# Weight splits of 1024 columns and adaLN modulation in units of 1024 columns, in a two-layer hybrid mixer step

## The chip, the cores and the metric

The kernel runs on one core of a Trainium2 chip. The metric is the time of one execution on the device in microseconds; the median of three runs before the change is 1260.74 us (1260.21 to 1266.0). TensorE is PE in the profile (PEld its weight loads), VectorE is DVE, ScalarE is ACT, SyncE is SP; SP issues the large loads.

## The reference

Two token groups (128 prompt tokens, 256 sample tokens) pass through two layers of width D = 2048. Each layer's modulation is a matrix product of a conditioning vector with `w_mod`; its three parts of 2048 columns are shift, scale and gate.

```python
def trunk_layer(x, cvec, l, p, rope=None, ctx_k=None, ctx_v=None):
    shift, scale, gate = jnp.split(jax.nn.silu(cvec) @ p['w_mod'][l] + p['b_mod'][l], 3, axis=-1)
    h = rmsnorm(x, p['norm_g'][l]) * (1 + scale) + shift
    (f_x, f_g, p_x, p_g, q, k, v, a_g, c_a, c_b, c_g) = jnp.split(h @ p['w_in'][l], N_IN_CHUNKS, axis=-1)
    y_f = fourier_mix(f_x, p['w_fourier'][l]) * jax.nn.silu(f_g)
    y_p = pool_mix(p_x, p['w_pool'][l], p['pool_scale'][l]) * jax.nn.silu(p_g)
    y_c = conv_module(c_a, c_b, ...) * jax.nn.silu(c_g)
    ...
    y_a = o.transpose(0, 2, 1, 3).reshape(b, s, D_BRANCH) * jax.nn.silu(a_g)
    y = jnp.concatenate([y_f, y_p, y_a, y_c], axis=-1) @ p['w_out'][l]
    return x + gate * y, k, v
```

The prompt group has one conditioning vector and the sample group another, so every modulation is computed for two vectors. All data are float32. After the second layer a last rmsnorm gives the outputs; the prompt's keys and values are outputs too.

## The kernel before

**Matrix products.** The 384 tokens of both groups stand in the free dimension, and D in 16 blocks of 128 partitions (KC = 16). A weight tile is 512 KB, [128 partitions x 2 blocks x 512 columns], in a pool of five buffers (`rawp`). `wtile` (L219) loads it and `halves` (L203) splits each half of 512 columns into a rounded part `hi` (ACT, `copy_a`, L115) and a rest `lo` (DVE, `tt`, L106), in pools of six buffers each. `mm3` (L428) then does three matmuls of 384 columns for each 128 x 128 block: `hh`x`hi` (L429), `hl`x`hi` (L430), `hh`x`lo` (L431), where `hh` and `hl` are the two parts of the activation (`yh`, `yl` in the output projection). A tile has 24 such matmuls (`main_tile`, L433). In the trace each of them is one record where it reads rounded data, and two where it reads plain float32.

**Stages of a layer.** Eleven chunks of 512 columns of `w_in`, the mixers between them, then the output projection with `w_out`. Layer 0's first four chunks run differently: they are taken k-group by k-group (nine groups, four tiles each) while the modulation of layer 0 is still being computed; `make_h` makes the activation of a group (`ht`, `hh`, `hl`), and DVE adds each tile's result from PSUM into `acc`. Which instruction comes when on an engine is settled by the scheduler of the Tile framework; loads and splits go into it with priority (`ahead`, L200).

**Modulation.** It is doled out beside the main work. `pump` (L341) runs after each weight tile and issues what is due of two lists.
- *PE items* (`mod_item`, L247): a load of `mraw` and, for each block of 128 rows and each of four groups of 32 columns of the PE array, one matmul (L271) with the conditioning vectors (`cmod`) as the stationary side, into PSUM `mod`. Two items are issued at a time (BP = 2). An item of two blocks with 512 columns has eight matmuls of 128 columns; one of one block with 1024 columns has four of 256. At a unit's end a transpose (`T`) and `mod_store` follow.
- *DVE side items* (`side_item`, L307): a load of `sraw` [128 x 2 x 512], then for each of the two blocks and both vectors one DVE instruction of 512 columns into `macc` (L321 for the first block, L109 after it). When all 16 blocks are in, eight matmuls with ones (`mds`, L331), 128 columns each, sum over the partitions, then a transpose and `mod_store` follow. `macc` and `sraw` are taken from the pool `X` of four buffers in layer 0, and from the pool `H` in the output projection.

`share` (L374) assigns units to the two lists. For layer 1's shift and scale (L814) there are eight units of 512 columns: the first three go to PE, NS = 5 to DVE. For layer 1's gate (L941) there are four, two of them (NG = 2) on DVE; the two on PE are merged into one wide unit (`mod_wide`). How fast the lists go is set by tile counts (PE0, PE1, DV0, DV1 in L64).

**The layer boundary.** After layer 0's last output tile TensorE does the last `mds`, the first wide unit of layer 1's gate (16 matmuls), sums of squares (`st`, L412), a broadcast (`bc`, L407), and then layer 1's first matmuls as soon as `hh` is there.

Of the kernel before, what the change touches and what calls it, by code (L numbers as in the profile page):

```python
# [14 lines left out]
P = 128  # L15
# [40 lines left out]
def mixer_step(  # L56
# [8 lines left out]
    NS, NG = 5, 2  # L65
# [13 lines left out]
    hip = ctx.enter_context(tc.tile_pool(name="hip", bufs=6))  # L79
    lop = ctx.enter_context(tc.tile_pool(name="lop", bufs=6))  # L80
# [56 lines left out]
    nc.vector.memset(cmod, 0.0)  # L137

# [64 lines left out]
    def halves(raw, src, widths):  # L203
        flat = raw.rearrange("p a b -> p (a b)") if len(raw.shape) == 3 else raw
        hs, ls = [], []
        with ahead():
            nc.sync.dma_start(out=src[0], in_=src[1])
        for i, w in enumerate(widths):
            hi = hip.tile([P, 512], F32R, tag="hi", name=nm("hi"))
            lo = lop.tile([P, 512], F32R, tag="lo", name=nm("lo"))  # L210
            r = flat[:, 512 * i:512 * i + w]
            with ahead():
                copy_a(hi[:, :w], r)
                tt(lo[:, :w], r, hi[:, :w].bitcast(F32), ALU.subtract)
            hs.append(hi)
            ls.append(lo)
        return hs, ls

    def wtile(src, nk=None, shape=(P, 2, 512)):  # L219
        nk = nk or shape[1]  # L220
        n = shape[2]
        raw = rawp.tile(list(shape), F32, tag="raw", name=nm("raw"))
        hs, ls = halves(raw, (raw[:, :nk], src), [min(512, nk * n - o) for o in range(0, nk * n, 512)])

        def part(ts):
            def at(j, cs=slice(0, n)):
                i, o = divmod(j * n, 512)
                return ts[i][:, o + cs.start:o + cs.stop]
            return at
        return part(hs), part(ls)  # L230
# [70 lines left out]
    def side_items(l, kind, b0):  # L301
        return [(l, kind, b0, k0) for k0 in range(0, KC, 2)]
# [4 lines left out]
    def side_item(l, kind, b0, k0):  # L307
        pool = side_pool[0]
        key = (l, kind, b0)
        if k0 == 0:  # L310
            side_acc[key] = gtile(pool, "macc", (P, 2, 512))
        acc = side_acc[key]
        raw = gtile(pool, "sraw", (P, 2, 512))
        c0 = MOD.index(kind) * D + b0 * P
        with ahead():
            nc.sync.dma_start(out=raw, in_=w_src("w_mod", l, k0, c0))
        for j in range(2):
            for v in range(2):
                cv = cmod[:, k0 + j, v:v + 1]
                if k0 + j == 0:  # L320
# [758 lines left out]
```

## Time and profile before

| | |
|---|---|
| median of the runs | 1260.74 us (1260.21, 1260.74, 1266.0) |
| the profiled execution | 1261.78 us, span 1260.0 us, mean granted TensorE clock 0.993 |
| TensorE busy | 98% of the span |
| VectorE busy | 72% |
| ScalarE busy | 44% |
| DMA | 251.85 MB moved, mean 200 GB/s |

The span is what the instructions of the profiled execution cover; the execution's own time is 1.78 us longer. Busy time is the union of an engine's records, and a group's mean is the length of one record: records of an engine overlap, so the distance between two starts (the pitch) is shorter than the mean. In the timeline a row of several records gives the start of the first, the time from there to the end of the last, and their count.

### The profile page before, as it was taken

What the parts mean: (1) busy time and instruction counts of PE and PEld (TensorE: products, weight loads), DVE (VectorE), ACT (ScalarE), POOL (GpSimd) and SP (SyncE); (2) the same over time, 40 slices, a digit from 0 to 9 for tenths busy, and PEclk for the clock granted to TensorE, in tenths of its full rate; (3) what the DMA queues carried; (4) which work ended last, traced back from release to release, by engine and by line L of the source; (5) the groups of instructions that cost most, each with busy time, mean ns of one, the idle gap of its engine ahead of it and who ended that gap; (6) DMA issues with size and microseconds to landing.
All of it is one profiled execution on the core that took longest, in us unless ns stands there. A gap on an engine that the chain in (4) does not pass through costs nothing.

```text
span 1260.0 us, 22153 instructions
## 1 busy us (share of the span) xinstructions
PE 1232.5 (98%) x8600; PEld 1155.2 (92%) x8600; DVE 912.3 (72%) x1773; ACT 553.7 (44%) x1116; POOL 2.1 (0%) x34
## 2 busy tenths in 40 slices
PE   7999999999999999999999999999999999999995
PEld 7789998798998999999998999979999999999995
DVE  0578777999975966998977559998455795647452
ACT  3423233345447545433235533334554765344442
POOL 0000000000000000000000000000000000000000
PEclk9999999999999999999999999999999999999998
DMA  5878887553446765888954444444323573545322
GB/s 222 317 295 324 289 328 269 189 186 113 139 150 226 273 241 185 314 307 318 329 198 176 165 153 159 153 159 147 103 84 118 175 243 117 192 162 189 118 68 100
DMA packets 70712, 251.85 MB, mean 200 GB/s; under 512 B 7760, under 2 KB 8912, under 8 KB 70608
## 3 DMA queue, kind: packets, MB, share of 16 engines
q1 hardware_dynamic: 70608, 250.45, 56.6%
q8 instruction: 67, 1.10, 0.4%
q14 instruction: 37, 0.30, 0.1%
HBM read 243.08 MB, written 7.34 MB: 199 GB/s over the span
## 4 chain that ended last, share of the span: by engine, by line
PE 92%; DVE 3%; DMA 2%; ACT 1%; issue 1%; SPq 0%; DVEq 0%; ACTq 0%
PE mm L429 25%; PE mm L430 23%; PE mm L431 23%; PE mod L271 5%; PE mm L460 2%; PE mm L461 2%; PE mm L462 2%; PE ssq L166 2%; DVE lo L106 1%; DMA raw<-in_w_in_dram 1%; PE sp L430 1%; PE sp L429 1%; PE scs L634 1%; PE sp L431 1%; PE aso L658 1%; PE fb L701 1%
## 5 line engine op out<-in xcount | busy, mean ns | idle before, releaser
L115 ACT ACTIVATE hi<-raw 128x512 fp32r<-128x512 f32 x498 | 308.4, 630 | 539.5 <-PE mm L430 340.8
L106 DVE TENSOR_TENSOR lo<-raw,hi 128x512 fp32r<-128x512 f32 x498 | 337.4, 687 | 209.4 <-ACT hi L115 198.9
L429 PE MATMUL mm<-hh,hi 128*128 128x384 f32 x1280 | 441.0, 345 | 5.4 <-ACT hh L112 3.9
L430 PE MATMUL mm<-hl,hi 128*128 128x384 f32 x1280 | 433.0, 338 | 0.0
L431 PE MATMUL mm<-hh,lo 128*128 128x384 f32 x1280 | 430.9, 338 | 0.4 <-DVE lo L106 0.4
L429 PEld LDWEIGHTS mm<-hh,hi 128*128 128x128 f32 x1280 | 241.0, 188 | 26.7 <-issue 11.4
L430 PEld LDWEIGHTS mm<-hl,hi 128*128 128x128 f32 x1280 | 242.1, 189 | 1.4 <-issue 0.6
L431 PEld LDWEIGHTS mm<-hh,lo 128*128 128x128 f32 x1280 | 241.5, 189 | 1.5 <-DVE lo L106 1.2
L429 PE MATMUL mm<-yh,hi 128*128 128x384 f32 x512 | 173.4, 340 | 0.3 <-DVE xr L109 0.3
L430 PE MATMUL mm<-yl,hi 128*128 128x384 f32 x512 | 172.4, 337 | 0.0
L431 PE MATMUL mm<-yh,lo 128*128 128x384 f32 x512 | 172.3, 337 | 0.0
L109 DVE SCALAR_TENSOR_TENSOR macc<-sraw,cmod,macc 128x512 f32<-128x512 f32 x210 | 147.4, 743 | 7.0 <-DMA sraw<-in_w_mod_dram 7.0
L109 DVE SCALAR_TENSOR_TENSOR cacc<-u,cst,cacc 128x399 f32<-128x399 f32 x232 | 146.5, 631 | 7.6 <-ACT cacc L112 3.2
L429 PEld LDWEIGHTS mm<-yh,hi 128*128 128x128 f32 x512 | 96.2, 188 | 3.9 <-issue 3.3
L430 PEld LDWEIGHTS mm<-yl,hi 128*128 128x128 f32 x512 | 96.3, 188 | 0.0
L431 PEld LDWEIGHTS mm<-yh,lo 128*128 128x128 f32 x512 | 96.2, 188 | 0.0
L106 DVE TENSOR_TENSOR acc<-acc,mm 128x384 f32<-128x384 f32 x128 | 65.4, 551 | 26.8 <-PE mm L431 26.7
L271 PE MATMUL mod<-mraw,cmod 128*32 128x128 f32 (+2 forms) x1920 | 76.8, 294 | 0.4 <-DVE T L276 0.4
L271 PEld LDWEIGHTS mod<-mraw,cmod 128*32 128x32 f32 x1920 | 48.2, 112 | 22.8 <-issue 14.6
L112 ACT ACTIVATE hh<-ht,AB 128x128 fp32r<-128x128 f32 x64 | 26.9, 450 | 25.8 <-DVE ht L109 25.6
L460 PE MATMUL mm<-hi,hh 128*128 128x512 f32 x96 | 38.3, 399 | 0.0
L461 PE MATMUL mm<-lo,hh 128*128 128x512 f32 x96 | 38.0, 396 | 0.0
(205 smaller groups left out, 954.9 us busy)
## 6 DMA issues: line engine op xcount, KB each, us to landing
raw<-in_w_in_dram SPq DMA_DIRECT2D x172, 512.0 KB, 4.3
mraw<-in_w_mod_dram SPq DMA_DIRECT2D x136, 512.0 KB, 4.4
raw<-in_w_out_dram SPq DMA_DIRECT2D x64, 512.0 KB, 4.3
sraw<-in_w_mod_dram SPq DMA_DIRECT2D x56, 512.0 KB, 5.6
xT<-in_x_dram SPq DMA_DIRECT2D x4, 768.0 KB, 7.2
xr<-in_x_dram SPq DMA_DIRECT2D x4, 768.0 KB, 6.5
xd<-xr SPq DMA_DIRECT2D x4, 768.0 KB, 6.3
xr<-xd SPq DMA_DIRECT2D x4, 768.0 KB, 6.0
```

Source lines behind the costliest of these rows:

```text
L106: (eng or nc.vector).tensor_tensor(out=out, in0=a, in1=b, op=op)
L109: nc.vector.scalar_tensor_tensor(out=out, in0=a, scalar=s, in1=b, op0=op0, op1=op1)
L112: nc.scalar.activation(out=out, in_=a, func=func, **kw)
L115: nc.scalar.activation(out=out, in_=a, func=AF.Copy, scale=scale)
L166: nc.tensor.matmul(ssq[:, t:t + 1], lhsT=xsq[:, b, t * P:(t + 1) * P], rhs=ones[:, 0:1], start=g == 0 and b == 0 and t == 0, stop=g == 3 a ...
L271: nc.tensor.matmul(ps[qs, 0:nb * 32].rearrange("p (b n) -> p b n", n=32), lhsT=cmod[:, k0 + j, :], rhs=raw[:, j, :, qs], start=(k0 + j == ...
L429: nc.tensor.matmul(ps, lhsT=wh, rhs=ah, start=start, stop=False)
L430: nc.tensor.matmul(ps, lhsT=wh, rhs=al, start=False, stop=False)
L431: nc.tensor.matmul(ps, lhsT=wl, rhs=ah, start=False, stop=stop)
L460: nc.tensor.matmul(ps3[t], lhsT=hh[g][:, kb, ts], rhs=hi(j), start=st, stop=False)
L461: nc.tensor.matmul(ps3[t], lhsT=hh[g][:, kb, ts], rhs=lo(j), start=False, stop=False)
L462: nc.tensor.matmul(ps3[t], lhsT=hl[g][:, kb, ts], rhs=hi(j), start=False, stop=sp)
```

## The change

The split of a weight tile becomes one `hi` and one `lo` instruction of up to 1024 columns, with pools of three buffers of 1024 columns in place of six of 512. Modulation units for layer 1 have 1024 columns: four units for shift and scale, NS = 3 of them on DVE and one on PE, and two for the gate, NG = 1 on DVE and one on PE. A side item covers one block of 128 rows by 1024 columns: one load of 512 KB, two DVE instructions of 1024 columns; the sums for the two vectors stand in two tiles of the pool instead of one. At a unit's end eight matmuls of 256 columns have `pick` as the stationary side (a column of ones at the vector's place), and the two vectors accumulate into one tile.

```diff
--- before.py
+++ after.py
@@ -62,7 +62,7 @@
     nc = tc.nc
     PRIO = 1000
     PE0, PE1, DV0, DV1 = 78, 45, 61, 34
-    NS, NG = 5, 2
+    NS, NG = 3, 1
     WF, WP, WQ, WC = 3, 2, 3, 0
     YC1, YC2, YC3, YT = 1, 4, 1, 2
     NB1, NB2 = 2, 2
@@ -76,8 +76,8 @@
     pbp = ctx.enter_context(tc.tile_pool(name="pbp", bufs=4))
     cap = ctx.enter_context(tc.tile_pool(name="cap", bufs=1))
     rawp = ctx.enter_context(tc.tile_pool(name="rawp", bufs=5))
-    hip = ctx.enter_context(tc.tile_pool(name="hip", bufs=6))
-    lop = ctx.enter_context(tc.tile_pool(name="lop", bufs=6))
+    hip = ctx.enter_context(tc.tile_pool(name="hip", bufs=3))
+    lop = ctx.enter_context(tc.tile_pool(name="lop", bufs=3))
     kvp = ctx.enter_context(tc.tile_pool(name="kvp", bufs=2))
     tiny = ctx.enter_context(tc.tile_pool(name="tiny", bufs=2))
     tmpp = ctx.enter_context(tc.tile_pool(name="tmpp", bufs=2))
@@ -135,6 +135,10 @@
     nc.vector.memset(eps_t, EPS)
     cmod = one.tile([P, KC, 32], F32, tag="cmod", name="cmod")
     nc.vector.memset(cmod, 0.0)
+    pick = one.tile([P, 2, 32], F32, tag="pick", name="pick")
+    nc.vector.memset(pick, 0.0)
+    for v in range(2):
+        nc.vector.memset(pick[:, v, v:v + 1], 1.0)
 
 
     in_order = ExitStack()
@@ -200,34 +204,24 @@
     def ahead():
         return tc.high_priority(offset=PRIO if prio[0] else 0)
 
-    def halves(raw, src, widths):
-        flat = raw.rearrange("p a b -> p (a b)") if len(raw.shape) == 3 else raw
-        hs, ls = [], []
-        with ahead():
-            nc.sync.dma_start(out=src[0], in_=src[1])
-        for i, w in enumerate(widths):
-            hi = hip.tile([P, 512], F32R, tag="hi", name=nm("hi"))
-            lo = lop.tile([P, 512], F32R, tag="lo", name=nm("lo"))
-            r = flat[:, 512 * i:512 * i + w]
-            with ahead():
-                copy_a(hi[:, :w], r)
-                tt(lo[:, :w], r, hi[:, :w].bitcast(F32), ALU.subtract)
-            hs.append(hi)
-            ls.append(lo)
-        return hs, ls
-
     def wtile(src, nk=None, shape=(P, 2, 512)):
         nk = nk or shape[1]
         n = shape[2]
+        w = nk * n
         raw = rawp.tile(list(shape), F32, tag="raw", name=nm("raw"))
-        hs, ls = halves(raw, (raw[:, :nk], src), [min(512, nk * n - o) for o in range(0, nk * n, 512)])
-
-        def part(ts):
+        hi = hip.tile([P, 1024], F32R, tag="hi", name=nm("hi"))
+        lo = lop.tile([P, 1024], F32R, tag="lo", name=nm("lo"))
+        r = raw.rearrange("p a b -> p (a b)")[:, :w]
+        with ahead():
+            nc.sync.dma_start(out=raw[:, :nk], in_=src)
+            copy_a(hi[:, :w], r)
+            tt(lo[:, :w], r, hi[:, :w].bitcast(F32), ALU.subtract)
+
+        def part(t):
             def at(j, cs=slice(0, n)):
-                i, o = divmod(j * n, 512)
-                return ts[i][:, o + cs.start:o + cs.stop]
+                return t[:, j * n + cs.start:j * n + cs.stop]
             return at
-        return part(hs), part(ls)
+        return part(hi), part(lo)
 
     def w_src(name, l, k0, c0, nk=2, n=512):
         def rows(a):
@@ -299,39 +293,38 @@
         return mod_items(l, ((kind, k0, 8),), 1)
 
     def side_items(l, kind, b0):
-        return [(l, kind, b0, k0) for k0 in range(0, KC, 2)]
+        return [(l, kind, b0, k) for k in range(KC)]
 
     side_acc = {}
     side_pool = ["X"]
 
-    def side_item(l, kind, b0, k0):
+    def side_item(l, kind, b0, k):
         pool = side_pool[0]
         key = (l, kind, b0)
-        if k0 == 0:
-            side_acc[key] = gtile(pool, "macc", (P, 2, 512))
+        if k == 0:
+            side_acc[key] = [gtile(pool, "macc", (P, 1024)) for _ in range(2)]
         acc = side_acc[key]
-        raw = gtile(pool, "sraw", (P, 2, 512))
+        raw = gtile(pool, "sraw", (P, 1, 1024))
         c0 = MOD.index(kind) * D + b0 * P
         with ahead():
-            nc.sync.dma_start(out=raw, in_=w_src("w_mod", l, k0, c0))
-        for j in range(2):
-            for v in range(2):
-                cv = cmod[:, k0 + j, v:v + 1]
-                if k0 + j == 0:
-                    nc.vector.tensor_scalar(out=acc[:, v, :], in0=raw[:, j, :], scalar1=cv, scalar2=None, op0=ALU.mult)
-                else:
-                    stt(acc[:, v, :], raw[:, j, :], cv, acc[:, v, :], ALU.mult, ALU.add)
-        if k0 + 2 == KC:
+            nc.sync.dma_start(out=raw, in_=w_src("w_mod", l, k, c0, 1, 1024))
+        for v in range(2):
+            cv = cmod[:, k, v:v + 1]
+            if k == 0:
+                nc.vector.tensor_scalar(out=acc[v], in0=raw[:, 0, :], scalar1=cv, scalar2=None, op0=ALU.mult)
+            else:
+                stt(acc[v], raw[:, 0, :], cv, acc[v], ALU.mult, ALU.add)
+        if k + 1 == KC:
             del side_acc[key]
-            ps = sm("mds", (P, 2, 4, 32))
-            av = acc.rearrange("p v (b n) -> p v b n", n=P)
-            for v in range(2):
-                for q in range(4):
-                    qs = slice(32 * q, 32 * q + 32)
-                    nc.tensor.matmul(ps[qs, v], lhsT=ones[:, 0:32], rhs=av[:, v, :, qs])
-            T = one.tile([P, 2, 4, 32], F32, tag="S", name=nm("T"))
-            nc.vector.transpose(out=T.rearrange("p v b n -> p (v b n)"), in_=ps.rearrange("p v b n -> p (v b n)"))
-            mod_store(l, kind, b0, 4, T[:, :, :, 0].rearrange("p v b -> p b v"))
+            ps = sm("mds", (P, 8, 32))
+            for q in range(4):
+                qs = slice(32 * q, 32 * q + 32)
+                for v in range(2):
+                    nc.tensor.matmul(ps[qs], lhsT=pick[:, v, :], rhs=acc[v].rearrange("p (b n) -> p b n", n=P)[:, :, qs],
+                                     start=v == 0, stop=v == 1)
+            T = one.tile([P, 8, 32], F32, tag="S", name=nm("T"))
+            nc.vector.transpose(out=T.rearrange("p b n -> p (b n)"), in_=ps.rearrange("p b n -> p (b n)"))
+            mod_store(l, kind, b0, 8, T[:, :, 0:2])
 
     fill = {"pe": [], "dve": []}
     rate = {"pe": 0.0, "dve": 0.0}
@@ -373,12 +366,8 @@
 
     def share(l, units, n_side):
         n_pe = len(units) - n_side
-        for i in range(n_pe):
-            kind, b0 = units[i]
-            if i % 2 == 0 and i + 1 < n_pe and units[i + 1] == (kind, b0 + 4):
-                fill["pe"].extend(mod_wide(l, kind, b0))
-            elif not (i % 2 and units[i - 1] == (kind, b0 - 4)):
-                fill["pe"].extend(mod_items(l, ((kind, b0, 4),), 2))
+        for kind, b0 in units[:n_pe]:
+            fill["pe"].extend(mod_wide(l, kind, b0))
         for kind, b0 in units[n_pe:]:
             fill["dve"].extend(side_items(l, kind, b0))
 
@@ -811,7 +800,7 @@
             in_order.close()
             make_lambda()
             fill["pe"].extend(mod_wide(0, "gate", 0)[8:] + mod_wide(0, "gate", 8))
-            share(1, [(kind, b0) for b0 in range(0, KC, 4) for kind in ("shift", "scale")], NS)
+            share(1, [(kind, b0) for b0 in range(0, KC, 8) for kind in ("shift", "scale")], NS)
             set_rate("pe", PE0)
             src = {ci: (lambda b, ci=ci: acc[ci][:, b, :]) for ci in lead}
             th = glu_tanh(src[C_B], acc[C_B])
@@ -938,7 +927,7 @@
         pump(flush=True)
         rate["pe"] = rate["dve"] = 0.0
         if not final:
-            share(1, [("gate", b0) for b0 in range(0, KC, 4)], NG)
+            share(1, [("gate", b0) for b0 in range(0, KC, 8)], NG)
             pe_mods(NB1)
         stat = tots[1]
         if not final:
```

The scheduler orders the new program anew. In it the line numbers are smaller: `mod` is L265, `mds` L323, `mm3` L418 to L420, `st` L401, `bc` L396.

VectorE in the first four chunks of layer 0, around one weight tile, before (`ht` is the scaled activation of a block, `acc` the sum of a chunk in SBUF, the last two rows the two halves of one tile's split):

```order
L109 SCALAR_TENSOR_TENSOR ht_936<-xT_120,AB_204,bcs_218 128x128
L109 SCALAR_TENSOR_TENSOR ht_936<-xT_120,AB_204,bcs_218 128x256
L106 TENSOR_TENSOR acc_467<-acc_467,mm_835 128x384
L106 TENSOR_TENSOR acc_467<-acc_467,mm_836 128x384
L106 TENSOR_TENSOR acc_467<-acc_467,mm_837 128x384
L106 TENSOR_TENSOR acc_467<-acc_467,mm_838 128x384
L106 TENSOR_TENSOR lo_929<-raw_926,hi_928 128x512
L106 TENSOR_TENSOR lo_933<-raw_926,hi_932 128x512
```

Now:

```order
L109 SCALAR_TENSOR_TENSOR ht_924<-xT_124,AB_208,bcs_222 128x128
L109 SCALAR_TENSOR_TENSOR ht_924<-xT_124,AB_208,bcs_222 128x256
L109 SCALAR_TENSOR_TENSOR ht_931<-xT_124,AB_208,bcs_222 128x128
L109 SCALAR_TENSOR_TENSOR ht_931<-xT_124,AB_208,bcs_222 128x256
L106 TENSOR_TENSOR acc_471<-acc_471,mm_831 128x384
L106 TENSOR_TENSOR acc_471<-acc_471,mm_832 128x384
L106 TENSOR_TENSOR acc_471<-acc_471,mm_833 128x384
L106 TENSOR_TENSOR acc_471<-acc_471,mm_834 128x384
L106 TENSOR_TENSOR lo_920<-raw_918,hi_919 128x1024
```

Two `ht` of the next block have moved ahead of the four additions, and one `lo` of 1024 columns stands for two.

TensorE at the layer boundary, from the end of layer 0's output projection on, before (`mds` sums a side unit, `mod` is the gate's unit, `st` the sums of squares, `bc` the broadcast):

```order
L331 MATMUL mds_7217<-macc_6810,ones 32x128 x8
L331 MATMUL mds_7278<-macc_7229,ones 32x128 x8
L271 MATMUL mod_7293<-mraw_7291,cmod 32x256
L412 MATMUL st_7159<-ones,xsq_7205 128x1 x3
L271 MATMUL mod_7293<-mraw_7291,cmod 32x256 x3
L271 MATMUL mod_7293<-mraw_7298,cmod 32x256 x4
L271 MATMUL mod_7293<-mraw_7304,cmod 32x256 x4
L271 MATMUL mod_7293<-mraw_7310,cmod 32x256 x4
L407 MATMUL bc_7324<-dg_7320,ones 128x384
```

Now, from the last two of eight `mds` rows on (`macc_6304` and `macc_6305`, the sums of the two vectors, alternate):

```order
L323 MATMUL mds_6577<-macc_6304,pick 32x256
L323 MATMUL mds_6577<-macc_6305,pick 32x256
L265 MATMUL mod_6592<-mraw_6590,cmod 32x256 x4
L265 MATMUL mod_6592<-mraw_6597,cmod 32x256 x4
L265 MATMUL mod_6592<-mraw_6603,cmod 32x256
L401 MATMUL st_6487<-ones,xsq_6527 128x1 x3
L265 MATMUL mod_6592<-mraw_6603,cmod 32x256 x3
L265 MATMUL mod_6592<-mraw_6609,cmod 32x256 x4
L396 MATMUL bc_6623<-dg_6619,ones 128x384
```

One side unit ends there instead of two, and the three `st` have moved from behind the first `mod` to behind the ninth.

## Rows read from the trace of the kernel before

**Rows 1.** Page, head and part 1: engine busy us, share of the span, instructions.

```profile
span 1260.0 us, 22153 instructions
...
PE 1232.5 (98%) x8600; PEld 1155.2 (92%) x8600; DVE 912.3 (72%) x1773; ACT 553.7 (44%) x1116; POOL 2.1 (0%) x34
```

**Rows 2.** Page, part 4: the chain that ended last, by engine.

```profile
PE 92%; DVE 3%; DMA 2%; ACT 1%; issue 1%; SPq 0%; DVEq 0%; ACTq 0%
```

**Rows 3.** TensorE's waits: who for, us in total, times, longest.

```profile
PE ssq L166 <- ACT xsq L112: 6.8, 1, 6.8
PE mm L429 <- ACT hh L112: 3.9, 3, 1.9
...
PE mm L429 <- DVE acc L106: 1.3, 1, 1.3
...
PE mm L431 <- DVE lo L106: 0.4, 1, 0.4
```

**Rows 4.** Groups by line and form: shapes, count | busy us, mean ns | idle before.

```profile
L106 DVE TENSOR_TENSOR lo<-raw,hi 128x512 fp32r<-128x512 f32 x498 | 337.4, 687 | 209.4 <-ACT hi L115 198.9 <-PE mm L431 7.8 <-PE mm L430 1.4
...
L109 DVE SCALAR_TENSOR_TENSOR macc<-sraw,cmod,macc 128x512 f32<-128x512 f32 x210 | 147.4, 743 | 7.0 <-DMA sraw<-in_w_mod_dram 7.0
...
L106 DVE TENSOR_TENSOR rsh<-rsh,cst 128x1024 f32<-128x1024 f32 x4 | 4.9, 1215 | 0.0
```

**Rows 5.** TensorE's timeline, three bursts: start us, us, line, count.

```profile
509.47 0.65 PE L331 MATMUL mds<-macc,ones 128*32 128x128 f32 x16
...
536.16 0.34 PE L431 MATMUL mm<-yh,lo 128*128 128x384 f32 x1
...
537.44 0.44 PE L429 MATMUL mm<-yh,hi 128*128 128x384 f32 x1
...
710.51 0.34 PE L429 MATMUL mm<-hh,hi 128*128 128x384 f32 x1
710.68 0.34 PE L430 MATMUL mm<-hl,hi 128*128 128x384 f32 x1
710.86 0.34 PE L431 MATMUL mm<-hh,lo 128*128 128x384 f32 x1
711.13 1.07 PE L271 MATMUL mod<-mraw,cmod 128*32 128x256 f32 x16
712.13 0.45 PE L429 MATMUL mm<-hh,hi 128*128 128x384 f32 x1
```

**Rows 6.** Timelines of VectorE and TensorE in layer 0's output projection.

```profile
585.23 6.05 DVE L109 SCALAR_TENSOR_TENSOR macc<-sraw,cmod,macc 128x512 f32<-128x512 f32 x9
591.58 1.29 DVE L106 TENSOR_TENSOR lo<-raw,hi 128x512 fp32r<-128x512 f32 x2 [0.30 <-ACT hi L115]
...
597.70 0.44 PE L429 MATMUL mm<-yh,hi 128*128 128x384 f32 x1
```

**Rows 7.** Timelines of VectorE and TensorE, layer 0's first four chunks.

```profile
78.80 0.48 DVE L109 SCALAR_TENSOR_TENSOR ht<-xT,AB,bcs 128x256 f32<-128x256 f32 x1
...
81.30 1.29 DVE L106 TENSOR_TENSOR lo<-raw,hi 128x512 fp32r<-128x512 f32 x2
...
82.05 0.97 PE L431 MATMUL mm<-hh,lo 128*128 128x384 f32 x4
```

**Rows 8.** Window 500:660 (us; PE, PEld, DVE, ACT, POOL busy, clock, DMA), and side loads.

```profile
500.00:660.00 160.00, 159.70 (x1178) 153.36 (x1176) 143.45 (x253) 54.45 (x94) 0.35 (x6) 1.00 0.83 297
...
DMA to landing us min/median/max: 3.6/6.4/8.6
```

**Rows 9.** Layer boundary: TensorE's timeline, and the window's row.

```profile
676.03 1.07 PE L429 MATMUL mm<-hh,hi 128*128 128x384 f32 x4 [1.89 <-ACT hh L112]
...
678.25 0.52 PE L430 MATMUL mm<-hl,hi 128*128 128x384 f32 x1
678.57 0.52 PE L431 MATMUL mm<-hh,lo 128*128 128x384 f32 x1
...
660.00:680.00 20.00, 18.08 (x141) 15.66 (x141) 12.38 (x34) 8.26 (x17) 0.00 (x0) 0.92 0.60 219
```

## Prediction

> **What bounds the kernel now.** The reading goes from the page's engine line to the chain of waits, from there to TensorE's own waits, and only then to single stretches. TensorE (PE) is busy for 1232.5 of 1260.0 us [rows 1], and the chain that ended last lies on it for 92% [rows 2]. What it waits for by name is one startup wait of 6.8 us, 3.9 us in three pieces for ScalarE's (ACT's) `hh`, and little else; VectorE's (DVE's) `lo` accounts for 0.4 us, once [rows 3]. So the time is, to about 2%, TensorE's stream of matmuls at their pitch. A change shortens the kernel if it takes matmuls out of that stream or removes one of the few waits; a shorter list on DVE or ACT shortens nothing by itself.
>
> The profiled execution took 1261.78 us (span 1260.0 and 1.78 around it), 1.04 above the median of 1260.74. What follows are differences on that execution, and I set them against the median.
>
> **1. Splits of 1024 columns.** Each full weight tile had two `hi` and two `lo` instructions of 512 columns, now one of each. A 512-column `lo` takes 687 ns, and a subtract or multiply of 1024 columns in the trace takes 1215 ns [rows 4], so a tile's `lo` costs 1.22 us where it cost 1.37: 0.15 us x 249 tiles (498 halves) = 37 us of busy time by these means, less back to back. `hi` should fall likewise. All of that lies beside TensorE, so the saving is worth nothing. The cost is that `lo` comes later, and what hides it is how early `lo` is. In the busiest stretch a pair of `lo` is done at 592.87, and the tile's matmuls begin at 597.70 [rows 6], 4.8 us later. A `lo` that starts only when the whole `hi` is done, and is itself one piece, comes some 0.6 + 0.5 us later, and a buffer that is given back by the tile comes back half a tile later (12 matmuls of 0.17 us [rows 5], 2.1 us). Together 3.2 us, which fits. Were it gone, each tile would wait.
>
> It does not fit at the start, where layer 0's first four chunks run k-group by k-group and DVE adds every tile's result into SBUF. Two `lo` start at 81.30, and the first matmul that reads one runs at 82.05 [rows 7]: TensorE is there when the first half is done. One `lo` of 1024 columns is ready 1.22 us after its start, not about 0.7, so 0.5 later. The order of instructions also puts two more `ht` ahead of it, 0.48 us for the one of 256 columns [rows 7] and less for the one of 128, about 0.8 together; and it puts a mod item of 16 records (0.65 us, as the burst of that size [rows 5]) into TensorE's stream before the user, which hides half of this. Three tiles are that tight (near 65 and 81 us). I take +1.0 us; the ends are 0 (DVE's saving elsewhere brings it forward) and +4 (each of nine groups loses 0.45).
>
> Here a rule speaks against the change. The row shows no slack on an engine that is far from full over the span. The Trainium skill, Perfetto Trace Analysis, section Optimizing Scalar/DVE Operations, says that grouping helps an engine that is saturated, and that an engine which is not, but makes others wait, may do better with instructions broken up. By that rule this part only loses; by the rows it loses 1 us at the start and nothing later.
>
> **2. Modulation, TensorE's share.** Layer 1's shift and scale were 8 units of 512 columns, 3 on TensorE; now they are 4 of 1024, 1 on TensorE: 1536 columns against 1024. Before, 24 items stand in bursts of two; a burst takes 537.44 - 536.16 - 0.17 = 1.11 us out of the stream. After, 16 items of 1024 columns, in the form that layer 0's gate has already: 712.13 - 710.86 - 0.17 = 1.10 us a pair [rows 5]. Before: 12 pairs, two of them cut into pieces by the scheduler, 15.1 us in all. After: 8 pairs, one of them cut, 9.1 us; and a cut of the gate's burst among the Fourier matmuls near 297 us is gone (-0.7), so 8.4. Difference **-6.7 us**, all on the path.
>
> **3. Modulation, VectorE's share.** Each DVE unit ends in eight small matmuls (`mds`) that sum over partitions. There were seven units: five in the middle of the stream, 0.67 us each (0.65 by the records [rows 5]) or less inside a longer burst, 2.7 in sum, and two at the layer boundary. Now there are four, of 256-column matmuls: three in the stream and one at the boundary. Sixteen records of 256 columns took 1.07 us [rows 5]: 3 x 1.1 + 0.35 for one cut = 3.65. Difference **+0.95 us**.
>
> That holds if the order inside the burst is free. The old burst goes round the four column groups; the new one puts two matmuls (v = 0, 1) behind each other in one 32-column group. No row shows that. Lower end: 1.10, as in the gate's bursts. Upper end: each pass behind the last. 384 columns have a pitch of 0.17 us, so 256 need 0.115, and 16 records 1.85 and a start: 2.2, or +1.1 for each of three, +3.3. I take +0.5, nearer to the gate's row, since the two records of one instruction already follow each other in one group there.
>
> DVE's own load: macc of 512 columns come at 6.05 / 9 = 0.67 us [rows 6]. With the 528 ns that 512 more columns add [rows 4] one of 1024 comes at 1.20. Between 500 and 660 us DVE is busy for 143.45 of 160 [rows 8]. By the order that stretch had 120 macc (80 us) and will have 72 (86 us), while 34 tiles' `lo` save 2.4: 4 us more, so 90% goes to 92%. I cost it at 0; the cover is the 4.8 us above, and rival B is what happens without it.
>
> **4. Layer boundary.** TensorE waits 1.89 us for `hh`, and then its matmuls come 0.32 us apart for some 3.5 us; the granted clock over 660 to 680 is 0.92, so part of the stretch ran at 1.2 GHz [rows 9]. In the new order the three `st` stand behind nine mods instead of one (8 x 1.07 / 8 us [rows 5], so 1.1 us later in place), with seven after them instead of fifteen to hide the way from `st` to `bc`. Ends 0 and +1; I take +0.3.
>
> **Sum.** 1.0 - 6.7 + 0.95 + 0.5 + 0.3 = -3.95 us. Of the 1.7 us that TensorE waits for DVE's `acc` and `lo` [rows 3] I take off 0.3. That gives **1256.5 us**, 0.34% less. A measurement of this kernel can tell about 0.5% (6.3 us) from no change: below 1254.4 is faster, above 1267.0 slower, and the forecast lies between.
>
> **The rivals.**
> A. *Waits shrink too* (faster, 1250 to 1254). The waits of rows 3 other than the first are 5.6 us, and the slow pitch at the boundary costs another 1.6 (some 11 matmuls at 0.32 instead of 0.17 [rows 9]). If a freer DVE and ACT remove 3 to 6 of these 7, the time is 1250.5 to 1253.5. For it: both lists get shorter. Against: most of these waits end chains over several engines, which don't get shorter.
> B. *Two raw buffers feed VectorE too slowly* (slower, about 1268). The pool for the side work has four buffers: a unit held one for its sums and three for `sraw`, now two and two. A load is issued when a buffer is free and lands 6.4 us later (median [rows 8]); an item's two macc take 2.4. Two buffers thus give an item every (6.4 + 2.4) / 2 = 4.4 us, and the order wants 36 items in about 140 us, one each 3.9. The point from which it decides is a landing of 2 x 3.9 - 2.4 = 5.4 us. Then VectorE, which works in order, falls behind by 36 x 0.5 = 18 us, some 6 of it hidden by how early `lo` is: 1256.5 + 12 = 1268.5. For it: the median is past the point, and macc waited 7.0 us for `sraw` already [rows 4]. Against: the landing includes time behind other loads, which are fewer while SP waits; and with three buffers 7.0 us is little.
> C. *The two matmuls in one column group run one after the other* (no change). 3.3 instead of 0.5 and another 1.1 at the boundary: 1260.4. Of the groups' order the trace shows only that in the gate's burst a 256-column record takes 0.067 us on average [rows 5] where alone it would need 0.115: groups overlap. The Trainium skill, TensorE: Matmul & The Clock Gate, says that matmuls stay in program order and only weight loads move ahead; by that a pair of one group holds up the next group, and this rival comes true.
> D. *The start pays in every group* (no change): the upper end of part 1, +3, 1259.5; with C 1263.4.
>
> **How the numbers follow.** My forecast (1254.4 to 1259) 0.41; A 0.25; B 0.14, of which 0.11 above the bound; C 0.11; D, alone or with C, 0.09, of which 0.01 above it. So faster 0.25, slower 0.12, the same 0.63. The range, 1250.5 to 1266.5, leaves out A's last part (0.06) and what lies above the bound (0.12).
>
> **What would show it.** Right: the page's mod rows of 128x128 fall by 384 records, `mds` is 64 records of 128x256 and its burst takes 1.1 us; TensorE's busy time falls by 4 to 6 us. Part 1 is wrong if TensorE waits over 2 us for `lo` before 120 us, part 3 if `mds` bursts take 2 us (C), and B is right if DVE's wait for `sraw` exceeds 15 us and TensorE idles between 500 and 660. If the time falls by more than 6.3 us, TensorE's waits must have shrunk (A).

## The result and the profile after

The changed kernel takes 1270.55 us (median of six runs, 1267.18 to 1272.99), the kernel before 1262.76 us (median of six runs, the first three among them). The ratio is 1.0068 with a 95% interval of 1.005 to 1.0085: slower, by some 8 us. The forecast was 1256.5 us and no change, the range ended at 1266.5. The profiled execution took 1271.96 us, with a span of 1270.2.

The page's head and part 1 of the changed kernel, and by engine the chain that ended last:

```profile
span 1270.2 us, 20602 instructions
...
PE 1234.8 (97%) x8296; PEld 1153.6 (91%) x8296; DVE 895.9 (71%) x1424; ACT 514.2 (40%) x872; POOL 2.1 (0%) x34
...
PE 86%; DVE 5%; DMA 4%; ACT 2%; issue 1%; SPq 0%; DVEq 0%; ACTq 0%
```

Against [rows 1, 2] VectorE has 16 us less to do, ScalarE 40 us less and TensorE 304 records less, and the span is 10.2 us longer. TensorE's busy time rose by 2.3 us although matmuls went, so some of them ran slower, and the chain now spends 11% on VectorE, DMA and ScalarE where it had 6%. TensorE's waits of the changed kernel say for what (columns as in [rows 3]):

```profile
PE ssq L170 <- ACT xsq L112: 6.2, 1, 6.2
PE mm L418 <- ACT hh L112: 5.9, 5, 2.0
PE bc L396 <- DVE dg L394: 4.0, 2, 3.7
PE scs L623 <- ACT pt L112: 1.7, 1, 1.7
PE sp L418 <- ACT csh L115: 1.4, 1, 1.4
...
PE mm L420 <- DVE lo L106: 1.0, 2, 0.5
PE mm L418 <- DVE acc L106: 0.6, 1, 0.6
PE sp L419 <- DVE csl L106: 0.5, 1, 0.5
```

Three kinds of wait are new against the kernel before: `bc` for `dg`, `sp` for `csh` and `csl`, `scs` for `pt`. A total doesn't tell where time is lost. For that I follow one event through both timelines, the start of the last matmul that reads a tile's `hi`, and subtract:

| weight tile, and where it stands | before, us | after, us | after - before |
|---|---|---|---|
| 0, the first | 38.43 | 37.83 | -0.60 |
| 35, end of the first four chunks | 213.69 | 215.45 | +1.76 |
| 128, the last of layer 0 | 668.64 | 667.87 | -0.77 |
| 129, layer 1 has begun | 681.57 | 681.19 | -0.38 |
| 210, in layer 1's last chunk but one | 1057.80 | 1057.80 | 0.00 |
| 214, after the convolution's projection | 1075.09 | 1085.63 | +10.54 |
| 253, the last | 1245.20 | 1255.35 | +10.15 |

At 1058 us the two kernels are level, after smaller losses and gains; then 10.5 us go within four tiles, at the convolution's tail in layer 1. There its layer norm ends (`rs`, `dg`, the broadcast `bc`, `u`), and the split result (`csh`, `csl`) goes into a small projection (`sp`). TensorE's timeline of the changed kernel there:

```profile
1059.19 0.34 PE L418 MATMUL mm<-hh,hi 128*128 128x384 f32 x1
1063.18 1.65 PE L396 MATMUL bc<-dg,ones 128*128 128x384 f32 x2 [3.66 <-DVE dg L394]
...
1066.23 0.52 PE L418 MATMUL mm<-hh,hi 128*128 128x384 f32 x1
1066.55 0.52 PE L419 MATMUL mm<-hl,hi 128*128 128x384 f32 x1
...
1071.12 0.79 PE L418 MATMUL sp<-csh,hi 128*128 128x384 f32 x3 [1.43 <-ACT csh L115]
1072.44 0.69 PE L419 MATMUL sp<-csl,hi 128*128 128x384 f32 x1 [0.53 <-DVE csl L106]
```

And VectorE's, with the two rows of the kernel before for `rs` and `dg` shown first:

```profile
1055.58 0.18 DVE L399 RECIPROCAL rs<-sq 128x3 f32<-128x3 f32 x1 [0.88 <-ACT sq L112]
1055.79 0.68 DVE L405 TENSOR_SCALAR dg<-cst,rs 128x128 f32<-128x128 f32 x3
```

```profile
1052.66 1.28 DVE L109 SCALAR_TENSOR_TENSOR macc<-sraw,cmod,macc 128x1024 f32<-128x1024 f32 x1 [0.99 <-DMA sraw<-in_w_mod_dram]
1053.87 1.22 DVE L106 TENSOR_TENSOR lo<-raw,hi 128x1024 fp32r<-128x1024 f32 x1
1055.00 2.64 DVE L109 SCALAR_TENSOR_TENSOR macc<-sraw,cmod,macc 128x1024 f32<-128x1024 f32 x2
1057.56 1.22 DVE L106 TENSOR_TENSOR lo<-raw,hi 128x1024 fp32r<-128x1024 f32 x1
1058.70 1.28 DVE L109 SCALAR_TENSOR_TENSOR macc<-sraw,cmod,macc 128x1024 f32<-128x1024 f32 x1
1059.89 0.17 DVE L388 RECIPROCAL rs<-sq 128x3 f32<-128x3 f32 x1
1061.26 1.28 DVE L109 SCALAR_TENSOR_TENSOR macc<-sraw,cmod,macc 128x1024 f32<-128x1024 f32 x1 [1.20 <-DMA sraw<-in_w_mod_dram]
1062.46 0.67 DVE L394 TENSOR_SCALAR dg<-cst,rs 128x128 f32<-128x128 f32 x3
```

Before, `dg` follows `rs` at once. Now macc of the gate's unit stand ahead of `rs` and between `rs` and `dg`, and two of them wait for their load first (0.99 and 1.20 us). So `dg` is 6.7 us later and TensorE, which had its spare tiles in front of it, waits 3.66. After that wait its matmuls come 0.32 us apart, some 13 of them, and again behind the wait for `csh`. The windows show it: granted clock 0.83, so part of the stretch at 1.2 GHz, where the same work before had 1.00.

```profile
1057.00:1087.00 30.00, 24.38 (x112) 22.75 (x111) 20.72 (x31) 15.37 (x26) 0.00 (x0) 0.83 0.48 166
```

```profile
1057.00:1076.00 19.00, 19.00 (x110) 18.73 (x109) 12.88 (x25) 15.17 (x29) 0.00 (x0) 1.00 0.27 94
```

(Changed kernel first.) `csh` is late for a second reason, as ScalarE's timeline shows: a `hi` that waits for TensorE to give back its buffer stands ahead of it.

```profile
1069.60 1.06 ACT L115 ACTIVATE hi<-raw 128x1024 fp32r<-128x1024 f32 x1 [3.43 <-PE mm L419]
1070.56 0.51 ACT L115 ACTIVATE csh<-u 128x384 fp32r<-128x384 f32 x1
```

By the distances between matmuls, 7.8 us of the changed kernel's tail are pauses (TensorE's own records show 5.6 us of them idle) and 2.9 us slow pitch, against 0.3 and 0.15 before.

Why is that work there? In the code, the gate's unit for VectorE is opened by `set_rate("dve", ...)` ahead of the convolution, and when the last chunk is through, `while any(k[0] == l for k in side_acc): side_item(...)` finishes an open unit, because its pool is wanted by the output projection. Before, the unit in progress had eight items, and the second unit waited for the output projection. A unit of 1024 columns has sixteen items, and all sixteen now fall ahead of it. By the code, the rate (16 items on 34 weight tiles) gives out seven items in the 16 tiles between the two places, in either kernel; the loop then adds one before and nine now.

### The profile page after: what moved, and what is told of

Its sections match the earlier page's. It is cut to its first block, busy times and chain, and to the rows that moved or that the text cites. A ratio compares the mean times of both kernels' runs of the same rounds, so it can differ in the third digit from the quotient of the medians.

```text
span 1270.2 us, 20602 instructions
## 1 busy us (share of the span) xinstructions
PE 1234.8 (97%) x8296; PEld 1153.6 (91%) x8296; DVE 895.9 (71%) x1424; ACT 514.2 (40%) x872; POOL 2.1 (0%) x34
## 3 DMA queue, kind: packets, MB, share of 16 engines
q8 instruction: 65, 1.06, 0.3%
## 4 chain that ended last, share of the span: by engine, by line
PE 86%; DVE 5%; DMA 4%; ACT 2%; issue 1%; SPq 0%; DVEq 0%; ACTq 0%
PE mm L418 23%; PE mm L420 22%; PE mm L419 22%; PE mod L265 4%; DMA raw<-in_w_in_dram 3%; DVE lo L106 2%; PE mm L449 2%; PE mm L450 2%; PE mm L451 2%; PE ssq L170 2%; PE scs L623 1%; PE sp L419 1%; ACT hi L115 1%; PE sp L420 1%; PE sp L418 1%
## 5 line engine op out<-in xcount | busy, mean ns | idle before, releaser
L115 ACT ACTIVATE hi<-raw 128x1024 fp32r<-128x1024 f32 (+1 forms) x254 | 264.6, 1043 | 528.6 <-PE mm L419 373.8
L106 DVE TENSOR_TENSOR lo<-raw,hi 128x1024 fp32r<-128x1024 f32 (+1 forms) x254 | 304.3, 1200 | 213.9 <-ACT hi L115 212.7
L418 PE MATMUL mm<-hh,hi 128*128 128x384 f32 x1280 | 442.3, 347 | 6.6 <-ACT hh L112 5.9
L420 PE MATMUL mm<-hh,lo 128*128 128x384 f32 x1280 | 433.0, 340 | 1.0 <-DVE lo L106 1.0
L418 PEld LDWEIGHTS mm<-hh,hi 128*128 128x128 f32 x1280 | 242.5, 190 | 28.0 <-issue 14.2
L420 PEld LDWEIGHTS mm<-hh,lo 128*128 128x128 f32 x1280 | 242.9, 190 | 2.4 <-DVE lo L106 1.8
L418 PE MATMUL mm<-yh,hi 128*128 128x384 f32 x512 | 173.8, 340 | 0.0
L420 PE MATMUL mm<-yh,lo 128*128 128x384 f32 x512 | 171.7, 336 | 0.0
L109 DVE SCALAR_TENSOR_TENSOR macc<-sraw,cmod,macc 128x1024 f32<-128x1024 f32 x120 | 149.3, 1278 | 14.4 <-DMA sraw<-in_w_mod_dram 14.2
L418 PEld LDWEIGHTS mm<-yh,hi 128*128 128x128 f32 x512 | 96.2, 188 | 4.8 <-ACT hi L115 3.3
L420 PEld LDWEIGHTS mm<-yh,lo 128*128 128x128 f32 x512 | 96.2, 188 | 0.0
L265 PE MATMUL mod<-mraw,cmod 128*32 128x128 f32 (+2 forms) x1664 | 71.1, 306 | 0.4 <-DVE T L270 0.4
L265 PEld LDWEIGHTS mod<-mraw,cmod 128*32 128x32 f32 x1664 | 41.7, 113 | 22.9 <-issue 13.2
```

The costliest lines, as they stand in the source:

```text
L106: (eng or nc.vector).tensor_tensor(out=out, in0=a, in1=b, op=op)
L109: nc.vector.scalar_tensor_tensor(out=out, in0=a, scalar=s, in1=b, op0=op0, op1=op1)
L115: nc.scalar.activation(out=out, in_=a, func=AF.Copy, scale=scale)
L265: nc.tensor.matmul(ps[qs, 0:nb * 32].rearrange("p (b n) -> p b n", n=32), lhsT=cmod[:, k0 + j, :], rhs=raw[:, j, :, qs], start=(k0 + j == ...
L418: nc.tensor.matmul(ps, lhsT=wh, rhs=ah, start=start, stop=False)
L420: nc.tensor.matmul(ps, lhsT=wl, rhs=ah, start=False, stop=stop)
```

## The experiments

Theory T: the sixteen items that must be finished sit in VectorE's order ahead of `rs`, `dg` and `csl`. Rivals: R1, the long splits hold up ScalarE and VectorE wherever they stand; R2, the two raw buffers (the two tiles for `sraw` that pool `X` has left beside the sums) starve VectorE. The last three columns are the change of TensorE's lag against the kernel before, from the profiled execution, by the tiles of the table above: from tile 0 to 35, from 35 to 128, and from 210 to 214. Each ratio is to the kernel before on the same chip. A column is one execution of each kernel. Five groups of runs have the same order of instructions up to layer 1's gate unit (the kernel before and e3; the changed kernel, e1 and e7; e2 and e5; e4 and e10; e6 and e9), and within them the first two columns differ by up to 1.5 us: less than that says nothing there.

| run | median, us | ratio, 95% | start | rest of layer 0 | tail |
|---|---|---|---|---|---|
| changed kernel | 1270.55 | 1.0068 [1.005, 1.0085] | +2.4 | -2.5 | +10.5 |
| e1 gate unit late | 1262.22 | 0.9996 [0.9985, 1.0006] | +3.7 | -2.3 | +0.2 |
| e2 splits of 512 | 1264.06 | 1.0008 [0.9994, 1.0022] | +1.3 | -2.4 | +3.6 |
| e3 before, unit forced | 1266.28 | 1.0039 [1.0022, 1.0055] | 0.0 | +1.3 | +4.3 |
| e4 before, splits of 1024 | 1264.83 | 1.0024 [1.001, 1.0037] | +1.5 | -0.2 | +0.2 |
| e5 late, splits of 512 | 1260.08 | 0.9992 [0.9978, 1.0006] | +1.2 | -3.6 | 0.0 |
| e6 halves, one buffer | 1264.58 | 1.0015 [1.0001, 1.0029] | +0.2 | -5.7 | +8.2 |
| e7 one raw load | 1265.63 | 1.0026 [1.0013, 1.0039] | +2.2 | -3.7 | +3.1 |
| e8 late, halves at the start | 1260.10 | 0.9985 [0.9972, 0.9999] | +0.3 | -2.3 | +0.2 |
| e9 late, halves everywhere | 1260.32 | 0.9989 [0.9977, 1.0001] | -0.4 | -4.7 | +2.1 |
| e10 before, forced, splits of 1024 | 1270.20 | 1.006 [1.0039, 1.0082] | +2.2 | -1.2 | +4.3 |
| e11 macc of 512 | 1273.37 | 1.0078 [1.0055, 1.0101] | +2.8 | -0.1 | +9.9 |

**e1.** The unit is opened where the output projection begins.

```diff
-        set_rate("dve", (DV0, DV1)[l])
+        if l == 0:
+            set_rate("dve", DV0)
         y = conv(l, u)
...
         side_pool[0] = "H"
+        if l == 1:
+            set_rate("dve", 16)
```

> The changed kernel, but layer 1's gate unit on VectorE is opened only when the output projection starts, so that none of its 16 items has to be finished in front of the convolution's tail. Theory T (the forced 16 items sit in VectorE's order ahead of rs, dg and csl, and TensorE waits for these between 1058 and 1086 us): the 10.5 us that this stretch lost come back, about 1260 us, and the wait of bc for dg (3.7 us) is gone. Rival R1 (instructions of 1024 columns in the splits hold up ACT and DVE, whatever else they do): the stretch still loses most of it, 1267 us or more. Rival R2 (the two raw buffers): macc moves into the output projection with its waits for sraw, and TensorE waits there instead: 1265 or more.

1262.22 us; the tail's loss is gone, and of TensorE's waits these are left of the four in question:

```profile
PE scs L623 <- ACT pt L112: 1.7, 1, 1.7
...
PE bc L396 <- DVE dg L394: 0.4, 1, 0.4
```

T holds for the place: with the unit gone from there, and with splits of 1024 columns as in the changed kernel, there is no loss at the tail, so R1 can't be the cause by itself. R2 is not tested by this run. The unit now takes its tiles from pool `H`, of eight buffers, and the trace shows up to five of its loads issued and not yet used, where the changed kernel has two.

**e2.** Splits and their buffers of 512 columns again, units of 1024.

```diff
-        hi = hip.tile([P, 1024], F32R, tag="hi", name=nm("hi"))
-        lo = lop.tile([P, 1024], F32R, tag="lo", name=nm("lo"))
...
+        for o in range(0, w, 512):
+            e = min(512, w - o)
+            hi = hip.tile([P, 512], F32R, tag="hi", name=nm("hi"))
+            lo = lop.tile([P, 512], F32R, tag="lo", name=nm("lo"))
```

> The changed kernel with the splits back at 512 columns (two hi and two lo a tile, six buffers each); the modulation units stay at 1024 columns. T: the tail is still lost, only the start gains, 1 to 3 us: 1268 us. R1: the loss goes, 1258 to 1261 us. R2: no change, 1270 us.

1264.06 us, between the two. The tail loses 3.6 us instead of 10.5, which T did not expect: the long splits make the forced unit dearer. The trace has no more than two of the unit's loads out at once here too, so two raw buffers alone don't cost the 10.5 us.

**e3.** The kernel before, with both gate units forced.

```diff
-        while any(k[0] == l for k in side_acc):
+        while any(k[0] == l for k in side_acc) or (l == 1 and fill["dve"]):
```

> The kernel before, with one edit: both of layer 1's gate units on VectorE (16 items of 512 columns, three raw buffers) must be finished before the output projection, as the one big unit must be in the changed kernel. T: TensorE waits at the convolution's tail, 5 to 10 us more than the kernel before: 1268 to 1272 us. R1 and R2: no change within 2 us, 1262 us, since neither the splits nor the number of raw buffers differ.

1266.28 us, a little below what T expected; 4.3 us are lost at the tail, with `bc` waiting 2.0 us for `dg`. The forced work loses time in the old form too, with short splits. Three raw buffers were there by the code, but from 1026 us on the trace shows no more than two side loads out at once, so this is no run with three in use.

**e4.** The kernel before, with `wtile` and the pools of the changed kernel.

> The kernel before with the splits of 1024 columns alone (three buffers each); the modulation units stay at 512 columns. T: only the start loses, 1 to 3 us: 1264 to 1266 us. R1: most of the loss is there, 1268 to 1271 us. R2: no change, 1263 us.

1264.83 us: +1.5 us at the start, +0.2 at the tail. R1 alone falls, and the long splits are a small loss by themselves.

**e5.** e1 and e2 together.

> Both edits of the first two runs in the changed kernel: the gate unit opened at the output projection, and splits of 512 columns. If the losses are those two and the units of 1024 columns themselves gain (4 us on TensorE, as the run with splits of 512 columns showed between the end of the first four chunks and layer 1): 1257 to 1259 us, 4 below the kernel before. If the units gain nothing by themselves: 1262 us.

1260.08 us; the interval holds 1. Of the 4 us that were expected 1.8 came by the medians, 1.0 by the ratio.

**e6.** Two instructions each, one buffer.

```diff
-            copy_a(hi[:, :w], r)
-            tt(lo[:, :w], r, hi[:, :w].bitcast(F32), ALU.subtract)
+            for o in range(0, w, 512):
+                e = min(w, o + 512)
+                copy_a(hi[:, o:e], r[:, o:e])
+                tt(lo[:, o:e], r[:, o:e], hi[:, o:e].bitcast(F32), ALU.subtract)
```

> The changed kernel with two instructions of 512 columns for hi and two for lo, but still into one buffer of 1024 columns (three of each). It parts the length of the instruction from the size of the buffer. If the length holds up what stands behind it on ACT and DVE: as with splits and buffers of 512 columns, 1263 to 1265 us. If the buffer that comes back by the tile holds up hi, and csh behind it on ACT: as the changed kernel, 1269 to 1271 us.

The median, 1264.58, is that of short splits, but the columns part the two effects, and the total alone would have misled. The start recovers (+0.2): there the length of the instruction costs, or the order that the scheduler makes of it. In the rest of layer 0 (-5.7) a loss of 3.2 us in the attention is gone (more on it below). e2 and e5, with short splits in short buffers, don't have that loss either, but lose 2.7 and 1.6 us in layer 0's output projection, for a cause that stays open; so this column gives no price for the length. The tail (+8.2) does not recover: there it is mostly the buffers.

**e7.** The unit's loads but the first are left out; the first block's data stand for all sixteen.

```diff
-            nc.sync.dma_start(out=raw, in_=w_src("w_mod", l, k, c0, 1, 1024))
+            src = w_src("w_mod", l, k, c0, 1, 1024)
+            if not (l == 1 and kind == "gate" and k):
+                nc.sync.dma_start(out=raw, in_=src)
```

> The changed kernel, but layer 1's gate unit on VectorE loads only its first block and uses it for all 16 (15 loads of 512 KB and their waits are left out; the DVE instructions are the same). If the two raw buffers cause the loss at the tail (the waits for sraw of 1.0 and 1.2 us between 1052 and 1062 us stand ahead of dg): 2 to 7 us of the 10.5 come back, 1264 to 1268 us. If the macc themselves ahead of dg and csl cause it: 1269 to 1271 us.

1265.63 us; the tail loses 3.1 us. All the unit's macc are still there (the scheduler has put two more of them ahead of `rs`), and 7.5 of the 10.5 us go when they don't wait for loads. What is left is mostly the waits for `csh` (1.4 us) and `csl` (0.5). VectorE's timeline of this run has `dg` 1.3 us behind `rs`, not 2.6, and `rs` itself 3.3 us earlier (1.2 of it the lead that this execution has there anyway):

```profile
1056.63 0.17 DVE L394 RECIPROCAL rs<-sq 128x3 f32<-128x3 f32 x1
1056.71 1.25 DVE L109 SCALAR_TENSOR_TENSOR macc<-sraw,cmod,macc 128x1024 f32<-128x1024 f32 x1
1057.89 0.67 DVE L400 TENSOR_SCALAR dg<-cst,rs 128x128 f32<-128x128 f32 x3
```

The loads hang on the splits. SP issues weights and side loads in one order, in this stretch by turns, and waits for VectorE in both; of the changed kernel between 1020 and 1085 us:

```profile
SPq L216 <- DVE lo L106: 34.9, 13, 6.2
SPq L310 <- DVE macc L109: 11.3, 7, 3.0
```

A weight load waits until `lo` has freed a raw tile, `lo` waits for `hi`, and `hi` for a buffer that TensorE gives back. With a buffer of 1024 columns that is a whole tile later, and the `sraw` load behind it is late, then macc, then `dg`. That the buffers act along this way fits e2, e6 and e7, but each link was not tried by itself. Without the side loads the weight loads come sooner too, so e7 doesn't part the two. A third raw buffer in the changed kernel, the direct test of R2, was not tried.

**e8.** e1, and two instructions a split in the first four chunks alone (`sw = w if prio[0] else 512`).

> The changed kernel with the gate unit opened at the output projection, and in layer 0's first four chunks alone two instructions of 512 columns per split into the same buffers. If the start's loss (2.4 us to the 34th tile) comes from a lo of 1024 columns in front of ht on DVE: 1.5 to 2.5 us below the run with the late gate unit alone, 1260 us. If it comes from the buffers: no change, 1262 us.

1260.10 us; the start loses 0.3 us, not 3.7. The loss at the start is the long instruction, with its order. One of the places is the chain from the modulation's matmuls (`mod`, ending at 140.84 us, 140.02 before) over their transpose `T` to `ht`. ScalarE and VectorE, first the changed kernel, then the kernel before:

```profile
140.73 1.06 ACT L115 ACTIVATE hi<-raw 128x1024 fp32r<-128x1024 f32 x1 [11.55 <-DMA raw<-in_w_in_dram]
141.82 1.23 DVE L106 TENSOR_TENSOR lo<-raw,hi 128x1024 fp32r<-128x1024 f32 x1 [2.27 <-ACT hi L115]
142.96 0.31 DVE L270 STREAM_TRANSPOSE T<-mod 128x128 f32<-128x128 f32 x1
...
144.78 1.01 DVE L109 SCALAR_TENSOR_TENSOR ht<-xT,AB,bcs 128x128 f32<-128x128 f32 x3
```

```profile
139.56 2.43 ACT L115 ACTIVATE hi<-raw 128x512 fp32r<-128x512 f32 x4 [9.68 <-DMA raw<-in_w_in_dram]
140.22 1.29 DVE L106 TENSOR_TENSOR lo<-raw,hi 128x512 fp32r<-128x512 f32 x2 [1.49 <-ACT hi L115]
141.43 0.31 DVE L276 STREAM_TRANSPOSE T<-mod 128x128 f32<-128x128 f32 x1
...
143.17 1.01 DVE L109 SCALAR_TENSOR_TENSOR ht<-xT,AB,bcs 128x128 f32<-128x128 f32 x3
```

`T` stands behind a `lo`. The `lo` of 1024 columns starts only when the whole `hi` of 1.06 us is done, and `T` comes 2.1 us behind `mod`, where it came 1.4 us behind it. From `T` to `ht` there is little difference (1.82 us, 1.74 before). The wait for `hh` behind `ht` grew from 0.4 to 1.2 us.

**e9.** e1 and e6 together.

> The changed kernel with the gate unit opened at the output projection and two instructions of 512 columns per hi and lo, into one buffer of 1024. The units of 1024 columns stay. If the long split costs by the length of its instruction (2.4 us at the start, 3.2 us in the attention of layer 0) and the forced unit costs the rest (10.5 us), all three go and the units' gain is left: 5 to 6 us below the kernel before, 1256 to 1257 us. If the size of the buffer had a price of its own: 1259 us or more.

1260.32 us, 4 us short of what was expected. The rest of layer 0 stands at -4.7, but the tail lost 2.1 (`csh` behind the two `hi` on ScalarE, TensorE waits 1.5 us for it), and in the output projection TensorE waits 2.3 us for `xr`, the residual, part of it just behind the unit's closing burst: the blocks that need this unit's gate are due when it is barely done. Putting the unit off has a price of its own here: from tile 214 to the last one e9 loses 2.2 us and e5 1.5, though e1 and e8 lose none.

**e10.** e3 and e4 together.

> The kernel before with both edits that hurt: the two gate units finished before the output projection, and splits of 1024 columns; units of 512 columns and three raw buffers as before. If the forced work and the long splits make the 10.5 us together, whatever the number of raw buffers: 8 to 11 us lost at the tail, 1272 us. If it takes the two raw buffers: about 4 us at the tail, as with the forced work alone, and the 2 us of the splits, 1268 us.

The median says 1270.20, the profiled execution 1267.48 with 4.3 us at the tail and the rest at the start and the boundary. The ratio is about what e3 and e4 make together (1.0039 and 1.0024). So by the trace, forced work and long splits in the form of the kernel before don't make 10 us at the tail; by the median they may, in the executions without a profile. As in e3, no more than two side loads are out at once from 1029 us on, so the number of raw buffers is not tried either. This one does not decide.

**e11.** Each macc as two of 512 columns.

```diff
+            for o in (0, 512):
+                a, b = acc[v][:, o:o + 512], raw[:, 0, o:o + 512]
```

> The changed kernel, but each macc of 1024 columns as two of 512 (same loads, same two raw buffers, four DVE instructions an item). If the length of a macc in front of rs and dg matters: 1.2 us or more less at the tail, and 1268 us or below. If the wait for its load matters and not its length: no gain, or some us more, since DVE has more to do: 1270 to 1274 us.

1273.37 us, and 9.9 us at the tail: shorter macc gain nothing. The order changed with them: none stands between `rs` and `dg` any more, but `rs` itself comes later, behind macc of which one waited 0.87 us for its load, and VectorE has more instructions to do. So the run speaks against the length of a macc, and that the loads count instead rests on e7.

## Why the prediction was wrong

**The step that failed** is in part 3. It costed VectorE's side work at 0 because nothing waits for it between 500 and 660 us, and looked at no other place. That stretch behaved as said: VectorE 146.18 us busy of 160 (forecast about 147.5), TensorE without a gap.

```profile
500.00:660.00 160.00, 160.00 (x1005) 150.34 (x998) 146.18 (x165) 48.50 (x60) 0.35 (x6) 1.00 0.87 308
```

But the gate's unit is side work too, and the sum had no term for it. The change doubles a unit's items, and a rule of the kernel that finishes an open unit turned that into sixteen items ahead of the tail where eight had been: +10.5 us, more than all gains.

**Rival B** had a mechanism of the kind that was found (two raw buffers, loads that come late to an engine working in order, and TensorE behind it) and nearly the total, 1268.5, but the wrong place, so the nearness of the total is luck. Its premise fails where it looked. Layer 0's output projection takes its side tiles from `H`, of eight buffers, and between 505 and 640 us the trace shows up to six side loads out at once. VectorE waited 7.5 us for them there, and TensorE not at all. Over the whole run its wait for `sraw` is 17.9 us, past the 15 that B named. Never more than two are out from 392 to 462 us, where TensorE waits no more than 0.3 us, and from 988 us to the tail. There leaving the loads out (e7) gave back 7.5 of the 10.5 us and short splits, with two loads out as well (e2), 6.9. By these two runs late loads cost most of it, together with the long splits, and where macc stand directly ahead of what TensorE waits for. B's chance, 0.14, was too low because the stretch with the most work was taken for the stretch with the least slack.

**Part 1** took +1.0 for the start; it measured +2.4 by the trace (e4 alone +1.5, e8 +0.3). The named place, `lo` ahead of the first matmul, costs 0.5 us twice, once more than before; the rest is mostly `hh`, late by the longer splits ahead of `ht`. "Nothing later" was wrong too. In layer 0's attention VectorE's order now has a sum of 2.89 us (`lsum`) and a `lo` of 1.22 ahead of the maximum `nmx` that a head's exponential `pt` needs; before, `lsum` came behind `nmx`. The changed kernel, then the kernel before:

```profile
352.99 2.89 DVE L521 TENSOR_REDUCE lsum<-u 128x384 f32<-128x1536 f32 x1
355.79 1.22 DVE L106 TENSOR_TENSOR lo<-raw,hi 128x1024 fp32r<-128x1024 f32 x1
...
360.17 0.17 DVE L627 TENSOR_SCALAR nmx<-nmx 128x2 f32<-128x2 f32 x1
...
361.15 0.48 PE L623 MATMUL scs<-kctx,acc 64*128 64x128 f32 x2 [1.70 <-ACT pt L112]
```

```profile
358.38 0.16 DVE L638 TENSOR_SCALAR nmx<-nmx 128x2 f32<-128x2 f32 x1
358.45 2.96 DVE L532 TENSOR_REDUCE lsum<-u 128x384 f32<-128x1536 f32 x1
```

So `pt` is late, TensorE waits 1.7 us for it, and 11 of its matmuls then come at 0.32 us (3.2 us in sum). In e2, e5, e6 and e9, with instructions of 512 columns, `lsum` stands behind `nmx` again and this loss is gone; it comes by the order that the scheduler makes of the long splits, and its size by the length alone is not shown. So the Trainium skill's rule in Perfetto Trace Analysis, Optimizing Scalar/DVE Operations, was right for this kernel, and the trace agrees: neither engine was full, both made TensorE wait, and breaking the instructions up again (e6) gave back 2 us at the start and, with the order, 3 in the attention.

**Part 2 and the first half of 3** held. The unit's closing burst of 256-column matmuls takes 546.19 - 544.90 - 0.17 = 1.12 us:

```profile
544.90 0.34 PE L420 MATMUL mm<-yh,lo 128*128 128x384 f32 x1
545.16 1.09 PE L323 MATMUL mds<-macc,pick 128*32 128x256 f32 x16
546.19 0.45 PE L418 MATMUL mm<-yh,hi 128*128 128x384 f32 x1
```

So rival C falls: two matmuls in one column group cost no more than the gate's order. All bursts of `mod` and `mds` together take 81.0 us of TensorE's stream against 85.8, a gain of 4.8 where 5.25 was forecast (6.7 less 0.95 and 0.5): a burst cut after its first matmul costs 0.67 us for that one with 256 columns, where I had counted 0.35.

**Part 4** can't be judged by one execution: the boundary (tile 128 to 129) lost 0.39 us, for +0.3, but e3, with the order of the kernel before there, gained 1.5, and e7, with that of the changed kernel, lost 1.9. **Rival A** did not come: waits for `hh` grew from 3.9 to 5.9 us. **D** came in part.

## What to carry to other kernels

Where a unit of side work is made larger, look for every place that finishes or drains a unit, and price the work that is then forced there; the place with the least slack on the path counts, not the stretch with the most work. Here fewer and longer instructions on engines that are not full brought nothing, and they lengthened short chains that they stood in, or that the new order put them into. Before a pool's size goes into a sum, look which pool serves that stretch, and count in the trace how many of its tiles are out. Where a total moves, follow one event through both traces before building a theory: here it put the whole loss within four tiles.

## What the runs showed of the hardware

TensorE's wait of 3.7 us cost half of itself again: the next 13 matmuls of 384 columns came at 0.32 instead of 0.17 us, 1.8 us (2.9 over the tail, with the second wait). In e2 and e3, whose waits for `dg` were 1.9 and 2.0 us, the trace shows next to no slow pitch behind them (0.0 and 0.15 us), which is part of why e2 lost 3.6 us where the changed kernel lost 10.5. Yet 1.7 us in the attention and 2.04 at the boundary were followed by it, and behind a wait of 4.0 us in e6 the slow pitch cost 1.0 us, so the length of the wait alone does not tell.
